# Two weight sums of a seven-product group made by accumulating transfers instead of a VectorE add, with four units loaded ahead and two more places for weights

## The chip, the cores and the metric

One core of one Trainium2 chip. The metric is the device time of one execution in microseconds (us); the kernel before was run three times for it. A profiled execution of the same program gives the trace that the views below are taken from.

## The reference, cut to what matters

A decoder layer on 256 tokens of width 2048, in float32:

```python
def swiglu(x, w_gu, w_down):
    g, u = jnp.split(x @ w_gu, 2, axis=-1)
    return (jax.nn.silu(g) * u) @ w_down

h = layer_norm(alpha * h + 0.5 * swiglu(h, w_ffn1_gu, w_ffn1_down), ...)
...   # token mixers: retention, windowed attention, their projections
h = layer_norm(alpha * h + mixed, ...)
h = layer_norm(alpha * h + 0.5 * swiglu(h, w_ffn2_gu, w_ffn2_down), ...)
ple = jax.nn.sigmoid(h @ w_ple_gate) * (p @ w_ple_proj)
h = layer_norm(alpha * h + ple, ...)
```

The change lies in the two products `x @ w_gu` (2048 by 11264 weights each), which the kernel calls `f1_gu` and `f2_gu`.

## The kernel before, in words

Every float32 operand is split in two parts, a high part rounded to the matmul's own type by a cast (`hi`) and the rest (`lo`); a product is then three matmuls, `al*bh + ah*bh + ah*bl` (`Sum.add`, lines 410 to 412). One matmul streams 512 columns.

**Blocks and units.** A gate and up product is cut into 11 blocks of output columns, each with 8 units of weights. A unit is 1 MB: four blocks of weights, 128 rows by 512, in one slot of 128 x 2048 float32. A plain unit (`Unit`, letter P) makes 8 products, 24 matmuls. A group of seven (`Seven`, letter S) makes the same result with 7 products, 21 matmuls, by a scheme of Strassen's kind: it needs sums of weight blocks and sums of activations. Block 0 has eight P; blocks 1 to 10 have four of each, in an order written out in `ORDERS`, mostly `PPSSPSSP`. The sevens of a block have `p` = 0 to 3 in that order, the plain ones 4 to 7.

**The work for one unit.** SyncE loads the unit with two transfers (`Unit.load`, line 200). For P, ScalarE casts it (`hf_gu`, line 204) and VectorE subtracts (`lf_gu`, line 208). For S, ScalarE casts three of the four weight blocks (`hbf_gu`, line 236). VectorE then makes four sums `u`: two with one add of 1024 elements (line 243), `u0 = b1 + b0` and `u1 = b2 + b0`, and one each at lines 247 and 248. ScalarE casts the sums in two halves (`huf_gu`, lines 244 and 249). VectorE makes the low parts `lb` (line 253, 1536 elements) and `lu` (line 257, 2048 elements). The add at 243 needs only the loaded blocks, and `lb` stands between the add at 248 and `lu`.

**What sets the order.** Each engine runs its instructions in the order in which the program emits them, and a planner in the kernel sets that order. It keeps two clocks, one for TensorE and one for VectorE (`spend` adds the time of an operation), and emits the steps of making a unit whenever the VectorE clock is behind. `load()` issues loads up to `room["far"]` units ahead, as far as `room["slots"]` places allow; `cast()` emits the next unit's first cast ahead of its turn where a place is free. `weights(n)` sets the number of places for each stage. All tiles of weights share a pool of 23 slots (`SLOTS`); in a gate and up block the planner is given `SLOTS - 5 - (j + 1) // 2` of them, 17 at block 1 and 13 at block 9, and two fewer in block 10. The rest hold the activation forms of the sevens (two slots), the block's output `eve` (one), the finished activations (`raws`, one for each two blocks).

**The end of a block.** At the last seven of a block the four auxiliary sums in PSUM are folded (`seven_common`): ScalarE copies one (line 496), VectorE does three operations (lines 499 to 501). Four pairs of PSUM banks are in rotation, and the next block's first matmuls write the pair that the fold reads last. Then VectorE adds the other two sums (line 831), ScalarE takes the silu (line 833), VectorE multiplies (line 836), and in the next block TensorE transposes the result (line 789) and ScalarE copies it out (line 790).

Of the kernel before, what the change touches and what calls it, by code (L numbers as in the profile page):

```python
# [8 lines left out]
F32 = mybir.dt.float32  # L9
F32R = mybir.dt.float32r  # L10
I32 = mybir.dt.int32
AF = mybir.ActivationFunctionType
ALU = mybir.AluOpType
PSUM = bass.MemoryType.PSUM

P = 128
S = 256
# [9 lines left out]
KF = FF // P  # L27
# [3 lines left out]
SLOTS = 23  # L31
# [65 lines left out]
    "b0, c0 b1, c1,, t0, t1,",  # L97
)

BIG = 3.0e38  # L100
MAGIC = 12582912.0
INV_2PI = 0.15915494309189535
# [20 lines left out]
def layer(ctx: ExitStack, tc: tile.TileContext, io):  # L123
    nc = tc.nc
    sync, act, dve, pe = nc.sync, nc.scalar, nc.vector, nc.tensor
# [3 lines left out]
    slots = ctx.enter_context(tc.tile_pool(name="slots", bufs=SLOTS))  # L129
# [7 lines left out]
    def slot(shape, dt, name):  # L137
        return slots.tile(shape, dt, tag="slot", name=name)
# [6 lines left out]
    plan = []  # L145
    GROUP_AT = {"rg": 8, "gr": 21, "ga": 29}

    class Place:


        def __init__(self, key):
            name, b, p = key
            self.grouped = True
            if name.endswith("_gu"):
                self.parts = [io[name][2 * b + c, :, p // 2, :, p % 2 * 2 : p % 2 * 2 + 2, :] for c in range(2)]
            elif name in GROUP_AT or name in ("w_ret", "w_att"):
                w, at = (io["w_in_f"], GROUP_AT[name]) if name in GROUP_AT else (io[name], 0)
                at += 4 * b
                self.parts = [w[at + c : at + 4 : 2, p // 2, :, p % 2 * 2 : p % 2 * 2 + 2, :] for c in range(2)]
            else:  # L160
                self.grouped = False
                self.parts = [io[name][2 * b + c, p] for c in range(2)]
# [9 lines left out]

        def piece(self, v, g, kk):
            return self.halves(v)[:, g, kk] if self.grouped else v[:, 2 * g + kk]

        def whole(self, raw):
            for c, src in enumerate(self.parts):
# [3 lines left out]
    def quarters(v):  # L181
        return v.rearrange("p j (c n) -> p j c n", c=2)

    class Unit:


        loads, makes, keeps, steps = 1, 2, 2, 1
# [9 lines left out]
        def load(self):  # L197
            self.tile()
            for dst, src in self.place.whole(self.raw):
                sync.dma_start(dst, src)  # L200
# [5 lines left out]
        def make(self):  # L206
            self.lo = slot([P, 4, 512], F32R, "l" + self.name)
            dve.tensor_tensor(self.lo, self.raw, self.hi, ALU.subtract)  # L208
            spend(2048)
            yield  # L210
# [18 lines left out]
    class Seven(Unit):  # L229


        loads, makes, keeps, steps = 1, 4, 4, 4
# [5 lines left out]
        def make(self):  # L238
            raw, hb, nm = self.place.blocks(self.raw), self.hb, self.name
            u = slot([P, 4, 512], F32, "u" + nm)  # L240
            hu = slot([P, 4, 512], F32R, "hu" + nm)
            at = quarters(u)
            dve.tensor_tensor(at[:, 0:2], raw[:, 1:3], raw[:, 0:1].broadcast_to([P, 2, 2, 256]), ALU.add)  # L243
            act.copy(hu[:, 0:2], u[:, 0:2])  # L244
            spend(1024)
            yield
            dve.tensor_tensor(at[:, 2], raw[:, 2], at[:, 0], ALU.add)
            dve.tensor_tensor(at[:, 3], at[:, 2], raw[:, 3], ALU.add)  # L248
            act.copy(hu[:, 2:], u[:, 2:])  # L249
            spend(512, 512)  # L250
            yield
            lb = slot([P, 3, 512], F32R, "lb" + nm)
            dve.tensor_tensor(quarters(lb), raw[:, 1:], quarters(hb), ALU.subtract)  # L253
            spend(1536)
            yield
            lu = slot([P, 4, 512], F32R, "lu" + nm)
            dve.tensor_tensor(lu, u, hu, ALU.subtract)  # L257
            spend(2048)
            self.b22, self.b11, self.b21 = ((hb[:, j], lb[:, j]) for j in range(3))
            self.t3, self.t1, self.t2, self.t4 = ((hu[:, j], lu[:, j]) for j in range(4))  # L260
            yield


# [1 line left out]
    clock = {"pe": 0.0, "dve": 0.0}  # L265
    loaded, making, ready = [], [], []
    beside = {}
    room = {"slots": 0, "used": 0, "far": 3}

    def spend(*sizes):  # L270
        for n in sizes:
            clock["dve"] += (n + 150) / 960
# [70 lines left out]
    def weights(n):  # L343
        room["slots"] = n
# [77 lines left out]
                    sums[t][c].add(half_of(lhs(2 * p + kk), t), u.piece(c, kk))  # L422

    def plan_block(name, b, units):
        plan.extend((Seven if kind == "S" else Unit)(name, b, p) for kind, p in units)

    def sums_of(ps, units):

# [7 lines left out]
    def block(name, b, units, lhs, forms, sums, fold, before=None, host=False):  # L436
        sevens = [p for kind, p in units if kind == "S"]
        aux = None
        for j, (kind, p) in enumerate(units):
            if before is not None:  # L440
                before(j)
            u = take(name, b, p)
            if kind == "P":
                for c in range(2):
                    for kk in range(2):
                        some_products(u, p, lhs, sums, (0, 1), (c,), (kk,))
                    if host and not c:
                        run_side()
                done(u)
                if (aux is None or not sevens) and j < len(units) - 1:  # L450
                    run_side()
                continue
            if aux is None:
                pair = [banks(f"{name}{b}s{j}") for j in range(2)]
                aux = p1, p6, p7, q5 = [Sum(pair[j // 2][:, j % 2], len(sevens)) for j in range(4)]
            a11, a12 = (half_of(lhs(2 * p + e), 0) for e in range(2))
            a22 = half_of(lhs(2 * p + 1), 1)
            f5, f6, f7, f3 = forms(p)
            q2, q3, q4 = sums[0][1], sums[0][0], sums[1][1]
            steps = [  # L460
                (p1, a11, u.b11), (q2, a12, u.b21), (q3, f3, u.b22), (q5, f5, u.t1),
                (p7, f7, u.t3), (p6, f6, u.t2), (q4, a22, u.t4),
            ]
            if p == sevens[-1]:
                steps = [steps[j] for j in (0, 3, 5, 4, 1, 2, 6)]
            for to, left, right in steps:
                to.add(left, right)
            done(u)
            if p == sevens[-1]:
                fold(*(x.ap for x in aux))  # L470
                sevens = []
# [301 lines left out]
    def ffn(name, i, ht, norm, keep, residual, keepers, away):  # L773
# [26 lines left out]
        for j in range(KF // 4):  # L800
            units = gu_units(name, j)
            if j:
                weights(SLOTS - 5 - (j + 1) // 2 - (2 if j == KF // 4 - 1 else 0))
            got = []
            offset = 0
            if norm is not None and j == 0:
                ps, sums = norm.front(name + "_gu", 0, rhs, units)
                offset, units = FRONT, units[FRONT:]
            else:
                ps = [banks(f"{name}g{j}{t}") for t in range(2)]  # L810
                sums = sums_of(by_half(ps), units)

            def before(u, j=j, offset=offset):
                u += offset
                if j == 3 and norm is None and u == 0:
                    load_constants()
                if j == 0 and norm is None and u == 6:
                    weights(12)
                if j == 0 and u == 7:
                    to = [slot([P, 16, P], F32R, f"{name}f{w}") for w in "hl"]  # L820
                    made["x"] = seven_forms(keep(), to)
                if j == KF // 4 - 1 and u in (4, 6):
                    convert(u // 2 - 2)

            block(name + "_gu", j, units, rhs, forms, sums, lambda *a: got.append(seven_common(*a)), before)
            if got:
                v = got[0]
                after()
                spend(1024, 1024)
                for t in range(2):  # L830
                    dve.tensor_tensor(v[:, 2 * t : 2 * t + 2], v[:, 2 * t : 2 * t + 2], ps[t], ALU.add)
                g, u = v[:, 0::2], v[:, 1::2]
                act.activation(g, g, AF.Silu)
                after(clock["dve"] + 1.3)
                spend(1024)
                dve.tensor_tensor(u, g, u, ALU.mult)
            else:
                v = slot([P, 4, 512], F32, f"{name}v{j}")
                u = v[:, 0::2]
                for t in range(2):  # L840
                    act.activation(v[:, 2 * t], ps[t][:, 0], AF.Silu)
                after(clock["pe"] + 1.2)
                spend(512, 512)
                for t in range(2):
                    dve.tensor_tensor(v[:, 2 * t], v[:, 2 * t], ps[t][:, 1], ALU.mult)
            later(1, lambda j=j, u=u: turned(j, u))
# [44 lines left out]
        units = second + [("P", p) for p in held]  # L891
# [779 lines left out]
```

## Time and profile before

| | |
|---|---|
| median of 3 runs | 2252.04 us (2251.95 to 2252.23) |
| the profiled execution's own time | 2252.07 us |
| its span, first to last instruction | 2250.2 us |
| TensorE busy | 2242.8 us |
| VectorE busy | 2025.6 us |
| ScalarE busy | 1221.1 us |
| GpSimd busy | 0.7 us |
| transfers | 465.31 MB, 207 GB/s over the span |

Busy time is a sum over instructions; TensorE's matmuls overlap one another in the pipeline, so that its busy time counts the time in which at least one is under way. Idle time of an engine that is not the bottleneck costs nothing. The DMA share is the mean busy share of the core's 16 DMA engines.

### The profile page before, as it was taken

The page shows a single profiled execution, that of the slowest core. Times are in us where ns is not written, and L with a number is a line of the kernel's source. Part 1 is how long each engine was busy: PE and PEld are TensorE (multiplying, and loading weights), DVE is VectorE, ACT ScalarE, POOL GpSimd, SP SyncE. Part 2 cuts the span into 40 slices and gives each one's busy share as a digit, 9 for nine tenths or more (in the row PEclk, how much of TensorE's full clock was granted, in tenths as well). Part 3 has the DMA queues.
Part 4 walks back from the last instruction along what each step waited for, and adds up shares of the span by engine and source line. Part 5 has one row for each costly group of instructions (what it writes and reads, how often), then busy time and mean ns, then how long its engine had stood idle before and what let it go on. Part 6 is the DMA issues. An engine that isn't in the chain of part 4 may idle for free.

```text
span 2250.2 us, 26572 instructions
## 1 busy us (share of the span) xinstructions
PE 2242.8 (100%) x10435; PEld 1870.6 (83%) x10435; DVE 2025.6 (90%) x1778; ACT 1221.1 (54%) x1030; POOL 0.7 (0%) x7
## 2 busy tenths in 40 slices
PE   9999999999999999999999999999999999999999
PEld 7888888888888888888888888888888888888887
DVE  7999999999997888899899878989999999989976
ACT  6655555555554455555555545455555566565542
POOL 0000000000000000000000000000000000000000
PEclk9999999999999999999999999999999999999999
DMA  8665665555577454355566665766566566555761
GB/s 318 206 214 179 214 206 186 190 204 206 210 271 264 166 221 150 137 197 193 168 210 220 195 215 195 271 230 216 174 206 213 185 201 207 187 213 214 281 268 70
DMA packets 189981, 465.31 MB, mean 207 GB/s; under 512 B 14368, under 2 KB 15904, under 8 KB 187296
## 3 DMA queue, kind: packets, MB, share of 16 engines
q1 hardware_dynamic: 188880, 462.43, 59.6%
q8 instruction: 82, 1.34, 0.2%
q10 hardware_dynamic: 976, 1.18, 0.2%
q14 instruction: 43, 0.35, 0.0%
HBM read 455.17 MB, written 8.39 MB: 206 GB/s over the span
## 4 chain that ended last, share of the span: by engine, by line
PE 99%; DMA 0%; DVE 0%; SPq 0%; ACT 0%; issue 0%; DVEq 0%; ACTq 0%
PE f1g L412 5%; PE f1g L410 5%; PE f1g L411 5%; PE f2g L411 4%; PE f2g L412 4%; PE f2g L410 4%; PE rqk L371 3%; PE aqk L371 2%; PE f2d L412 1%; PE f1d L411 1%; PE f2d L410 1%; PE f1d L410 1%; PE f1d L412 1%; PE f2d L411 1%; PE rqk L379 1%; PE f2e L412 1%
## 5 line engine op out<-in xcount | busy, mean ns | idle before, releaser
L208 DVE TENSOR_TENSOR lf_gu<-rf_gu,hf_gu 128x2048 fp32r<-128x2048 f32 x93 | 209.4, 2286 | 8.4 <-ACT hf_gu L204 8.4
L204 ACT CAST hf_gu<-rf_gu 128x2048 fp32r<-128x2048 f32 x93 | 175.9, 1909 | 34.4 <-DMA rf_gu<-in_f_gu 18.4
L257 DVE TENSOR_TENSOR luf_gu<-uf_gu,huf_gu 128x2048 fp32r<-128x2048 f32 x80 | 182.8, 2285 | 1.1 <-ACT huf_gu L249 1.1
L244 ACT CAST huf_gu<-uf_gu 128x1024 fp32r<-128x1024 f32 x80 | 84.2, 1053 | 141.8 <-DVE uf_gu L243 139.7
L412 PE MATMUL f1g<-lf_gu,xt 128*128 128x512 f32 x384 | 149.7, 390 | 0.5 <-DVE lf_gu L142 0.5
L410 PE MATMUL f1g<-hf_gu,xt 128*128 128x512 f32 x384 | 150.1, 391 | 0.1
L411 PE MATMUL f1g<-hf_gu,xt 128*128 128x512 f32 x384 | 149.7, 390 | 0.0
L208 DVE TENSOR_TENSOR lf_down<-rf_down,hf_down 128x2048 fp32r<-128x2048 f32 x60 | 136.2, 2287 | 13.5 <-ACT hf_down L204 5.5
L236 ACT CAST hbf_gu<-rf_gu 128x1536 fp32r<-128x1536 f32 x80 | 117.2, 1483 | 55.1 <-DMA rf_gu<-in_f_gu 40.2
L253 DVE TENSOR_TENSOR lbf_gu<-rf_gu,hbf_gu 128x1536 fp32r<-128x1536 f32 x80 | 140.1, 1751 | 0.0
L204 ACT CAST hf_down<-rf_down 128x2048 fp32r<-128x2048 f32 x60 | 114.3, 1913 | 47.5 <-DMA rf_down<-in_f_down 14.2
L410 PE MATMUL f2g<-hf_gu,ht 128*128 128x512 f32 x320 | 124.7, 390 | 0.0
L412 PE MATMUL f2g<-lf_gu,ht 128*128 128x512 f32 x320 | 124.7, 390 | 0.0
L411 PE MATMUL f2g<-hf_gu,ht 128*128 128x512 f32 x320 | 124.6, 390 | 0.0
L249 ACT CAST huf_gu<-uf_gu 128x1024 fp32r<-128x1024 f32 x80 | 84.2, 1052 | 34.2 <-DVE uf_gu L248 34.1
L243 DVE TENSOR_TENSOR uf_gu<-rf_gu 128x1024 f32<-128x1024 f32 x80 | 97.5, 1219 | 0.0
L412 PEld LDWEIGHTS f1g<-lf_gu,xt 128*128 128x128 f32 x384 | 72.1, 188 | 16.1 <-DVE lf_gu L142 1.2
L410 PEld LDWEIGHTS f1g<-hf_gu,xt 128*128 128x128 f32 x384 | 72.2, 188 | 15.3 <-ACT hf_gu L141 0.6
L411 PEld LDWEIGHTS f1g<-hf_gu,xt 128*128 128x128 f32 x384 | 72.3, 188 | 14.9
L257 DVE TENSOR_TENSOR luf_down<-uf_down,huf_down 128x2048 fp32r<-128x2048 f32 x28 | 64.0, 2287 | 7.8 <-ACT huf_down L249 5.9
L411 PEld LDWEIGHTS f2g<-hf_gu,ht 128*128 128x128 f32 x320 | 60.1, 188 | 12.4
L410 PEld LDWEIGHTS f2g<-hf_gu,ht 128*128 128x128 f32 x320 | 60.1, 188 | 12.4
(1331 smaller groups left out, 6418.6 us busy)
## 6 DMA issues: line engine op xcount, KB each, us to landing
rf_gu<-in_f_gu SPq DMA_DIRECT2D x350, 512.0 KB, 5.2
rf_down<-in_f_down SPq DMA_DIRECT2D x176, 512.0 KB, 4.5
rw_rv<-in_w_rv SPq DMA_DIRECT2D x32, 512.0 KB, 4.4
rrg<-in_w_in_f SPq DMA_DIRECT2D x32, 512.0 KB, 4.6
rgr<-in_w_in_f SPq DMA_DIRECT2D x32, 512.0 KB, 4.6
rw_ret<-in_w_ret SPq DMA_DIRECT2D x32, 512.0 KB, 5.0
rga<-in_w_in_f SPq DMA_DIRECT2D x32, 512.0 KB, 5.0
rw_mix<-in_w_mix SPq DMA_DIRECT2D x32, 512.0 KB, 4.5
```

Of the source, the lines that this page charges most:

```text
L204: act.copy(self.hi, self.raw)
L208: dve.tensor_tensor(self.lo, self.raw, self.hi, ALU.subtract)
L236: act.copy(quarters(self.hb), self.place.blocks(self.raw)[:, 1:])
L243: dve.tensor_tensor(at[:, 0:2], raw[:, 1:3], raw[:, 0:1].broadcast_to([P, 2, 2, 256]), ALU.add)
L244: act.copy(hu[:, 0:2], u[:, 0:2])
L249: act.copy(hu[:, 2:], u[:, 2:])
L253: dve.tensor_tensor(quarters(lb), raw[:, 1:], quarters(hb), ALU.subtract)
L257: dve.tensor_tensor(lu, u, hu, ALU.subtract)
L371: pe.matmul(ps[:, f], u.tile_of(kk)[0][:, f * P : (f + 1) * P], rhs(k), start=k == 0, stop=k == KD - 1,)
L410: pe.matmul(o, al, bh, start=first, stop=False)
L411: pe.matmul(o, ah, bh, start=False, stop=False)
L412: pe.matmul(o, ah, bl, start=False, stop=self.left == 0)
```

## The change

Sevens with `p` = 0 and `p` = 2 of `f1_gu` and `f2_gu` become `Summed`: two of the four in each of the ten blocks that have sevens, in both products, 40 units in all. Instead of the add at line 243, `u0` and `u1` are loaded as `b1` and `b2` by SyncE into a slot of their own, and two accumulating transfers issued by GpSimd add `b0` to each. `raw` then gets only `b1` to `b3`. In `make` the low part `lb` comes first and `lu` follows the second cast of the sums at once. `room["far"]` goes from 3 to 4 for the whole program, and each gate and up block after the first gets two more places; `SLOTS` stays at 23.

```diff
+SUMMED = [(name, p) for name in ("f1_gu", "f2_gu") for p in (0, 2)]
...
+        def block(self, g, kk):
+            name, b, p = self.key
+            if name.endswith("_gu"):
+                return io[name][2 * b : 2 * b + 2, g, p // 2, :, p % 2 * 2 + kk].rearrange("c p n -> p c n")
...
+        def half(self, g):
+            name, b, p = self.key
+            at = slice(p % 2 * 2, p % 2 * 2 + 2)
+            if name.endswith("_gu"):
+                return io[name][2 * b : 2 * b + 2, g, p // 2, :, at].rearrange("c p k n -> p c (k n)")
...
+    class Summed(Seven):
+        loads, makes, keeps, steps = 2, 3, 4, 3
+
+        def load(self):
+            self.tile()
+            self.u = slot([P, 4, 512], F32, "u" + self.name)
+            at, blocks = quarters(self.u), self.place.blocks(self.raw)
+            for j, place in enumerate(((0, 1), (1, 0))):
+                sync.dma_start(at[:, j], self.place.block(*place))
+            for j in range(2):
+                nc.gpsimd.dma_start(at[:, j], self.place.block(0, 0), accum_op=ALU.add)
+            sync.dma_start(blocks[:, 1], self.place.block(0, 1))
+            if self.place.grouped:
+                sync.dma_start(self.raw[:, 1::2], self.place.half(1))
+            else:
+                sync.dma_start(self.raw[:, 2:], self.place.parts[1])
+
+        def make(self):
+            raw, hb, nm, u = self.place.blocks(self.raw), self.hb, self.name, self.u
+            at = quarters(u)
+            lb = slot([P, 3, 512], F32R, "lb" + nm)
+            dve.tensor_tensor(quarters(lb), raw[:, 1:], quarters(hb), ALU.subtract)
+            spend(1536)
+            yield
+            hu = slot([P, 4, 512], F32R, "hu" + nm)
+            act.copy(hu[:, 0:2], u[:, 0:2])
+            dve.tensor_tensor(at[:, 2], raw[:, 2], at[:, 0], ALU.add)
+            dve.tensor_tensor(at[:, 3], at[:, 2], raw[:, 3], ALU.add)
+            act.copy(hu[:, 2:], u[:, 2:])
+            spend(512, 512)
+            yield
+            lu = slot([P, 4, 512], F32R, "lu" + nm)
+            dve.tensor_tensor(lu, u, hu, ALU.subtract)
+            spend(2048)
+            self.parts(hb, lb, hu, lu)
             yield
...
-    room = {"slots": 0, "used": 0, "far": 3}
+    room = {"slots": 0, "used": 0, "far": 4}
...
-        plan.extend((Seven if kind == "S" else Unit)(name, b, p) for kind, p in units)
+        for kind, p in units:
+            plan.append((Unit if kind == "P" else Summed if (name, p) in SUMMED else Seven)(name, b, p))
...
-                weights(SLOTS - 5 - (j + 1) // 2 - (2 if j == KF // 4 - 1 else 0))
+                weights(SLOTS - 3 - (j + 1) // 2 - (2 if j == KF // 4 - 1 else 0))
```

`parts` only names the finished tiles, as the end of `Seven.make` did.

More of the change, by code (lines that the diff above doesn't have):

```diff
@@ L151, in __init__ @@
         def __init__(self, key):
+            self.key = key
             name, b, p = key
@@ L174, in piece @@
             return self.halves(v)[:, g, kk] if self.grouped else v[:, 2 * g + kk]
+        def block(self, g, kk):
+            name, b, p = self.key
+            if name.endswith("_gu"):
+                return io[name][2 * b : 2 * b + 2, g, p // 2, :, p % 2 * 2 + kk].rearrange("c p n -> p c n")
+            if not self.grouped:
+                return self.parts[g][:, kk].rearrange("p (c n) -> p c n", c=2)
+            w, at = (io["w_in_f"], GROUP_AT[name]) if name in GROUP_AT else (io[name], 0)
+            at += 4 * b + 2 * g
+            return w[at : at + 2, p // 2, :, p % 2 * 2 + kk].rearrange("c p n -> p c n")
+        def half(self, g):
[3 more added lines that the diff above has]
+                return io[name][2 * b : 2 * b + 2, g, p // 2, :, at].rearrange("c p k n -> p c (k n)")
+            w, n = (io["w_in_f"], GROUP_AT[name]) if name in GROUP_AT else (io[name], 0)
+            n += 4 * b + 2 * g
+            return w[n : n + 2, p // 2, :, at].rearrange("c p k n -> p c (k n)")
         def whole(self, raw):
@@ L258, in make, with parts @@
             spend(2048)
+            self.parts(hb, lb, hu, lu)
+            yield
+        def parts(self, hb, lb, hu, lu):
             self.b22, self.b11, self.b21 = ((hb[:, j], lb[:, j]) for j in range(3))
             self.t3, self.t1, self.t2, self.t4 = ((hu[:, j], lu[:, j]) for j in range(4))
+    class Summed(Seven):
[26 more added lines that the diff above has]
+            spend(512, 512)
+            yield
+            lu = slot([P, 4, 512], F32R, "lu" + nm)
+            dve.tensor_tensor(lu, u, hu, ALU.subtract)
+            spend(2048)
+            self.parts(hb, lb, hu, lu)
             yield
```

## The prediction

> **What bounds the kernel now.** I read the page first, then the table of windows over the blocks of both gate and up products, then the waits of TensorE and of SyncE's queue, and last the timeline of VectorE and ScalarE through one change of blocks.
>
> ```profile
> span 2250.2 us, 26572 instructions
> PE 2242.8 (100%) x10435; PEld 1870.6 (83%) x10435; DVE 2025.6 (90%) x1778; ACT 1221.1 (54%) x1030; POOL 0.7 (0%) x7
> ...
> PE 99%; DMA 0%; DVE 0%; SPq 0%; ACT 0%; issue 0%; DVEq 0%; ACTq 0%
> ```
>
> ```profile
> PE idle L1551 <- POOL ident masks.py:199: 1.4, 1, 1.4
> PE pls L1484 <- DVE ends L1481: 1.2, 1, 1.2
> PE f1g L412 <- DVE lf_gu L142: 0.5, 1, 0.5
> ```
>
> The chain that ends last is 99% TensorE. TensorE is idle for 2250.2 - 2242.8 = 7.4 us in all, and the second fence, all its named waits, adds up to 3.1 us: at the start (L1551, L142) and in the last norm (L1484). The change touches none of them. The windows say the same of the place of the change (columns: stretch, length, then busy time and count of each engine, clock, DMA share, GB/s):
>
> ```profile
> 61.40:103.10 41.70, 41.70 (x192) 34.65 (x189) 41.29 (x31) 23.86 (x20) 0.00 (x0) 1.00 0.61 202
> ...
> sum 418.60, PE 418.60 PEld 347.81 DVE 402.40 ACT 239.75 POOL 0.00; mean PE 41.86 PEld 34.78 DVE 40.24 ACT 23.98 POOL 0.00
> ```
>
> ```profile
> sum 418.10, PE 418.10 PEld 347.41 DVE 398.82 ACT 238.88 POOL 0.00; mean PE 41.81 PEld 34.74 DVE 39.88 ACT 23.89 POOL 0.00
> ```
>
> The first row is one block, the sums are ten stretches in `f1_gu` and ten in `f2_gu`. TensorE is busy in all of each, at clock 1.00. VectorE is the second engine: 402.40 of 418.60 and 398.82 of 418.10, so 1.6 to 1.9 us free in each block. It keeps pace, but only just. The change alters no matmul. What it can do is keep TensorE fed or starve it; it cannot shorten it.
>
> **The add that goes, and the wait that comes.**
>
> ```profile
> L257 DVE TENSOR_TENSOR luf_gu<-uf_gu,huf_gu 128x2048 fp32r<-128x2048 f32 x80 | 182.8, 2285 | 1.1 <-ACT huf_gu L249 1.1
> L244 ACT CAST huf_gu<-uf_gu 128x1024 fp32r<-128x1024 f32 x80 | 84.2, 1053 | 141.8 <-DVE uf_gu L243 139.7
> ...
> L243 DVE TENSOR_TENSOR uf_gu<-rf_gu 128x1024 f32<-128x1024 f32 x80 | 97.5, 1219 | 0.0
> ```
>
> Forty of the eighty adds at 243 go: 40 x 1.219 = 48.8 us of VectorE, two in a block, 2.44 us. The order of the rest matters more than it looks. Timeline of VectorE, then of ScalarE, around the change from block 9 to 10 (start, length):
>
> ```profile
> 419.77 0.69 DVE L499 TENSOR_TENSOR eve<-eve,f_gu9s 128x512 f32<-128x512 f32 x1
> ...
> 421.28 1.22 DVE L501 TENSOR_TENSOR eve<-f_gu9s,eve 128x1024 f32<-128x1024 f32 x1
> 422.42 1.22 DVE L243 TENSOR_TENSOR uf_gu<-rf_gu 128x1024 f32<-128x1024 f32 x1
> 424.47 2.35 DVE L831 TENSOR_TENSOR eve<-eve,f1g 128x1024 f32<-128x1024 f32 x2 [0.83 <-PE f1g L412]
> ...
> 433.08 1.22 DVE L243 TENSOR_TENSOR uf_gu<-rf_gu 128x1024 f32<-128x1024 f32 x1
> 434.33 0.69 DVE L247 TENSOR_TENSOR uf_gu<-rf_gu,uf_gu 128x512 f32<-128x512 f32 x1
> 435.05 0.69 DVE L248 TENSOR_TENSOR uf_gu<-uf_gu,rf_gu 128x512 f32<-128x512 f32 x1
> 435.66 1.75 DVE L253 TENSOR_TENSOR lbf_gu<-rf_gu,hbf_gu 128x1536 fp32r<-128x1536 f32 x1
> 437.33 2.29 DVE L257 TENSOR_TENSOR luf_gu<-uf_gu,huf_gu 128x2048 fp32r<-128x2048 f32 x1
> 439.53 1.22 DVE L243 TENSOR_TENSOR uf_gu<-rf_gu 128x1024 f32<-128x1024 f32 x1
> ```
>
> ```profile
> 417.77 1.49 ACT L236 CAST hbf_gu<-rf_gu 128x1536 fp32r<-128x1536 f32 x1 [3.89 <-DMA rf_gu<-in_f_gu]
> 419.16 0.58 ACT L496 COPY eve<-f_gu9s 128x512 f32<-128x512 f32 x1
> ...
> 435.78 1.05 ACT L249 CAST huf_gu<-uf_gu 128x1024 fp32r<-128x1024 f32 x1 [0.34 <-DVE uf_gu L248]
> ```
>
> Now a seven takes VectorE from 433.08 to 439.53, 6.45 us. The second cast of the sums (L249) starts when the add at 248 is done and ends at 435.78 + 1.05 = 436.83; it is hidden under `lb` (L253), which is why `lu` has waited for it 1.1 us in total over 80. In `Summed`, `lb` comes first, so nothing lies between the add at 248 and `lu`: VectorE, free at 435.66, would wait until 436.83, 1.17 us. By these rows 40 x 1.17 = 46.8 us come back, and the net is 48.8 - 46.8 = 2 us of VectorE over twenty blocks: nothing. VectorE stays as loaded as before. The low bound of that wait is 0 (another step emitted there fills it), giving the full 2.44 us a block; the high bound adds a cast of the next unit that stands ahead on ScalarE, 1.49 us by L236. I take 1.17. The planner's own clock does not count the wait.
>
> The casts of ScalarE are the same in number; the first now waits for a transfer instead of L243.
>
> **Bytes.** A seven loads 4 blocks of 0.262 MB. A `Summed` loads two of them again and one twice by accumulation: 5 plain and 2 accumulating, +0.262 MB plain and +0.524 MB accumulating. In a block of two that is +0.52 and +1.05 MB; over 40 units HBM reads rise by 31.5 MB.
>
> ```profile
> 21.00:52.00 31.00, 31.00 (x139) 25.68 (x138) 25.81 (x18) 16.91 (x11) 0.00 (x0) 1.00 0.90 323
> ```
>
> A block now uses 0.61 of 41.7 us, 25.4 us, for 202 GB/s, so full use is 202 / 0.61 = 331 GB/s; this stretch near the start ran at 0.90 and 323 GB/s with TensorE busy throughout. At 331 GB/s the extra takes 1.58 us plain and 3.17 us if accumulating bytes cost as plain ones: share 0.72. No row shows an accumulating transfer, so the other end is where it saturates: 41.7 - 25.4 - 1.6 = 14.7 us for 1.05 MB, 71 GB/s, 4.6 times dearer than plain. I take a share between 0.72 and 0.80, the second if each such byte costs twice. The Trainium skill, "Collectives: The Full Stack", section "The bandwidth ceiling: the fold count and why AG ≠ RS ≠ AR", says that an adding transfer is slower not for the sum but for its two source reads, half the rate; by it the share is 0.80, and no run here shows it yet.
>
> **When the data is there.** Transfers and waits of SyncE:
>
> ```profile
> rf_gu<-in_f_gu ACTq DMA_DIRECT2D x2, 256.0 KB, 3.7
> rf_gu<-in_f_gu SPq DMA_DIRECT2D x2, 256.0 KB, 5.2
> ...
> L200 SPq DMA_DIRECT2D rf_gu<-in_f_gu x4: 368/418/470, 412.0 to 413.5; - x4
> ...
>   ACT hbf_gu L236: 5.0, 2
> ...
> DMA to landing us min/median/max: 3.8/5.6/7.3
> ```
>
> The last three rows are two units loaded from 412.0 on, the first of them a seven with `p` = 0, which will be `Summed`. Its add started at 422.42. `Summed` needs the sums one `lb` later, at about 424.1, 12.1 us after the load is issued. The chain: one issue of 0.42, a landing of 3.7 to 5.2, two issues on GpSimd (0.42 each as on SyncE, the nearest row), again 3.7 to 5.2: 8.7 to 11.7 us, in time. With 7.3 for each landing it is 15.9, 3.8 us late. Issue on GpSimd has no row; its low end is 0.42, and the chain bears 2.2 us for each with landings of 3.7. So no wait in my sum, 3.8 us at the far end.
>
> On SyncE four issues stand where two stood: 2 x 0.42 = 0.84 us more, and 0.262 MB more at 331 GB/s, 0.79 us; `raw` is complete 1.6 us later. Behind it in ScalarE's order wait the cast at 417.77 and the copy at 419.16 (L496), and behind that the fold, which ended at 421.28 + 1.22 = 422.50. The block's own first sum was complete only at 424.47, where L831 had waited 0.83 us for TensorE, and the next block writes the fold's banks after that. So the fold has 2.0 us to spare, and 1.6 leaves 0.4. Price on the path: 0, but this is the thinnest cover.
>
> **Places.** The pool keeps 23 slots, so "two more places" is room that lay unused in the planner's count, and a `Summed` in flight holds a slot more from load to `make`. With at most two in flight that is even: 0. `far` = 4 acts in every stage; a fourth load can take the place of a cast ahead, and VectorE then waits for that cast, as it already does now and then (idle before, last column):
>
> ```profile
> L208 DVE TENSOR_TENSOR lf_gu<-rf_gu,hf_gu 128x2048 fp32r<-128x2048 f32 x93 | 209.4, 2286 | 8.4 <-ACT hf_gu L204 8.4
> ```
>
> 8.4 us for 93 units, and even twice that is spread over two products and lies in VectorE's free time. 0, at most some 5 us.
>
> **Sum.** TensorE's path 2250.2 + 0 = 2250.2 us of span. The profiled execution took 2252.07, 1.9 more, and stands 0.03 above the median. Forecast 2252 us, no change; for this likeliest case 2249 to 2256.5. A measurement here can tell 0.2%, 4.5 us, from no change.
>
> **The rivals.**
> 1. Late sums or late folds: the wait moves to TensorE. Place: the first `Summed` of a block, its landing against ScalarE's copy L496 or the first cast of sums. It decides from the point where the fold is over 2.0 us later or VectorE loses over 1.6 to 1.9 us a block. With landings of 7.3 us, 3.8 - 1.7 = 2.1 us a block, 42 us, 2294; with half a microsecond a block, 10 us, 2262. For it: ScalarE already waits for the landing of such units (3.89 us), and VectorE gains nothing. Against: the second `Summed` of a block has more time, and loading further ahead may bring the first forward. Typical 2265.
> 2. The DMA engines saturate. Under 71 GB/s for accumulating bytes a block needs more than 41.7 us; at 50 GB/s 25.4 + 1.6 + 21.0 = 48.0, +6.3 us, 126 us over twenty blocks, 2378. Against: the engines have 39% free and two reads would leave 20%.
> 3. Writing descriptors on GpSimd holds VectorE. GpSimd is idle now (0.7 us). If each of four transfers a block stopped VectorE for its issue, 0.42 us by SyncE's row, the 1.7 us that are free would just cover it; at 1.25 us each it is 5.0 - 1.7 = 3.3 us a block, 66 us, 2318. Nearly all VectorE work here is two-input TENSOR_TENSOR. The Trainium skill, "SBUF — State Buffer", section "Who interferes with whom", has such an operation contend with GpSimd instructions that read SBUF, and infers that writing descriptors is not one; no run here shows it.
> 4. The change does less than it says, `far` = 4 alone acting: a few us of TensorE waits in the mixers, 2258.
> 5. Faster: TensorE's idle time is 7.4 us, so 2252.07 - 7.4 = 2244.7 is the floor, and none of it lies in the blocks; a gain of 4.6 us, 2247.5, would need most of it.
>
> **How the numbers follow.** No change 0.54. Rival 1 0.27, rival 2 0.07, rival 3 0.05, rival 4 0.05, rival 5 0.02. So faster 0.02, same 0.54, slower 0.44. The range goes from 2249 to 2282: it takes in the forecast, rival 4 and most of rival 1, and leaves out the far end of 1, and 2 and 3, under 0.2.
>
> **What the profile after would show.** Right: TensorE busy again for all of each block window; 40 instead of 80 adds at 1024 elements; `lu` of `Summed` waiting about 1.2 us for ScalarE's second cast, some 40 to 47 us in total, and VectorE's busy time down by 48.8; DMA share 0.72 to 0.80 in the blocks; GpSimd with 80 transfers. Wrong: TensorE waits on `luf_gu`, `huf_gu` or on the fold at the first matmuls of a block (rival 1), a DMA share near 1 (rival 2), longer VectorE operations beside GpSimd's work (rival 3). What would overturn the forecast is an accumulating transfer dearer or later than the plain rows say.

## The result, and the profile after

| | before | after |
|---|---|---|
| median of 4 runs | 2251.99 us (2251.80 to 2252.23) | 2389.15 us (2386.64 to 2394.14) |
| ratio | 1 | 1.0612, 95% interval 1.0592 to 1.0632 |
| the profiled execution's own time, span | 2252.07, 2250.2 us | 2394.14, 2392.4 us |

The change costs 137 us. The time after is outside the range of the prediction.

The functions moved down in the file: `Sum.add` is now at lines 478 to 480, a plain unit's cast and `lo` at 228 and 232, the old seven's operations at 260 to 281, `Summed`'s at 302 (SyncE), 304 (GpSimd), 315 (`lb`), 319 (first cast), 320 and 321 (sums), 322 (second cast) and 326 (`lu`), the fold at 565 to 570. The first lines of the page of the changed kernel, its two DMA queues (packets, MB, share) and its memory traffic:

```profile
span 2392.4 us, 26998 instructions
PE 2296.6 (96%) x10435; PEld 1890.4 (79%) x10435; DVE 1988.1 (83%) x1738; ACT 1220.0 (51%) x1030; POOL 98.9 (4%) x87
...
q1 hardware_dynamic: 210640, 472.92, 57.6%
q0 software_dynamic: 21760, 20.98, 5.8%
HBM read 486.62 MB, written 8.39 MB: 207 GB/s over the span
```

VectorE does less (2025.6 to 1988.1 us), the DMA engines are far from full, and TensorE executes the same 10435 matmuls. It is no longer busy all the time: idle 2392.4 - 2296.6 = 95.8 us where 7.4 were. That is 88.4 of the 142.2 us by which the span grew. The other 53.8 are busy time, the same matmuls taking longer. Windows over blocks 0 to 9 of the first product, from the transposes of block 0 to those of block 10, before and then after (columns: length, busy of TensorE, weight loads, VectorE, ScalarE, GpSimd, granted clock, DMA share, GB/s):

```profile
60.60:477.50 416.90, 416.90 (x1881) 346.41 (x1880) 402.30 (x300) 239.16 (x190) 0.00 (x0) 1.00 0.61 201
```

```profile
60.60:535.80 475.20, 438.32 (x1881) 354.25 (x1880) 385.89 (x280) 242.63 (x192) 44.15 (x36) 0.96 0.71 211
```

The same stretch of work takes 58.3 us longer. Of these 36.9 are idle and 21.4 busy, at a granted clock of 0.96. The same stretch of the second product grew by 60.6 us; the remaining 23 us lie mostly in the mixers between the two. What TensorE waited for, after (us in total, times, longest):

```profile
PE f1g L478 <- DVE eve L568: 19.5, 8, 5.0
PE f2g L478 <- DVE eve L568: 19.1, 6, 5.7
PE f1g L478 <- DVE eve L570: 8.7, 9, 1.1
PE f2g L478 <- DVE eve L570: 6.2, 8, 1.1
PE w_rv1s L480 <- DVE luw_rv L281: 3.5, 1, 3.5
PE w_mix1s L480 <- DVE lbw_mix L277: 2.9, 1, 2.9
```

The four largest, 53.5 us together, are one place: the first matmuls of a block, waiting for the fold of the block before. None of the larger waits is for weights of a `Summed`. Two more kinds, 15.9 us in seven waits, belong to the end of a block too: once the transposes wait for the other two sums (line 900), and six times matmuls of a seven in blocks 3, 4 and 6 wait for ScalarE's copy of the transposed result (line 859), as in

```profile
PE f2t L858 <- DVE eve L900: 2.9, 1, 2.9
PE f_gu3s L478 <- ACT f1a L859: 2.3, 1, 2.3
```

So the question is why the fold is late. VectorE's timeline around the fold of block 5, before and then after (start, length, engine, line, operation, in brackets the idle time before it and what ended it):

```profile
243.62 2.29 DVE L257 TENSOR_TENSOR luf_gu<-uf_gu,huf_gu 128x2048 fp32r<-128x2048 f32 x1
245.82 6.69 DVE L208 TENSOR_TENSOR lf_gu<-rf_gu,hf_gu 128x2048 fp32r<-128x2048 f32 x3
252.42 0.68 DVE L499 TENSOR_TENSOR eve<-eve,f_gu5s 128x512 f32<-128x512 f32 x1
```

```profile
262.79 2.29 DVE L232 TENSOR_TENSOR lf_gu<-rf_gu,hf_gu 128x2048 fp32r<-128x2048 f32 x1 [1.64 <-ACT hf_gu L228]
265.00 1.75 DVE L315 TENSOR_TENSOR lbf_gu<-rf_gu,hbf_gu 128x1536 fp32r<-128x1536 f32 x1
...
269.52 2.29 DVE L326 TENSOR_TENSOR luf_gu<-uf_gu,huf_gu 128x2048 fp32r<-128x2048 f32 x1 [1.45 <-ACT huf_gu L322]
271.73 1.22 DVE L267 TENSOR_TENSOR uf_gu<-rf_gu 128x1024 f32<-128x1024 f32 x1
...
275.99 2.28 DVE L281 TENSOR_TENSOR luf_gu<-uf_gu,huf_gu 128x2048 fp32r<-128x2048 f32 x1
278.19 0.68 DVE L568 TENSOR_TENSOR eve<-eve,f_gu5s 128x512 f32<-128x512 f32 x1
...
293.65 1.76 DVE L315 TENSOR_TENSOR lbf_gu<-rf_gu,hbf_gu 128x1536 fp32r<-128x1536 f32 x1 [5.99 <-PE f1g L479]
```

Before, three plain units stand ahead of the fold and the sevens of the next group come behind it. After, a whole `Summed` and a whole old seven stand ahead of it as well, with a wait for a cast in them. ScalarE's copy that the fold needs was made earlier, by 275.97 (275.39 + 0.58, ScalarE's timeline after); the fold started at 278.19, when VectorE came to it.

```profile
275.39 0.58 ACT L565 COPY eve<-f_gu5s 128x512 f32<-128x512 f32 x1
```

VectorE's row at 293.65 shows the other side of it: VectorE had run so far ahead that it then stood idle for 5.99 us until TensorE freed a slot. TensorE's timeline at the same moment:

```profile
273.57 0.39 PE L480 MATMUL f1g<-lf_gu,xt 128*128 128x512 f32 x1
278.93 0.69 PE L478 MATMUL f1g<-hf_gu,xt 128*128 128x512 f32 x1 [4.97 <-DVE eve L568]
...
281.56 0.63 PE L479 MATMUL f1g<-hf_gu,xt 128*128 128x512 f32 x1
281.99 0.63 PE L480 MATMUL f1g<-lf_gu,xt 128*128 128x512 f32 x1
...
286.33 0.40 PE L479 MATMUL f1g<-hf_gu,xt 128*128 128x512 f32 x1
286.56 0.40 PE L480 MATMUL f1g<-lf_gu,xt 128*128 128x512 f32 x1
```

It waits for 4.97 us, and the matmuls behind the wait start 0.43 us apart, until 285.8, where they start 0.23 us apart: half speed for about 7 us. Most of the 53.8 us of extra busy time is this: the granted clock of the profiled run is 0.981, and 0.019 of 2392.4 us are about 45 us.

How many units VectorE has finished when it comes to the fold can be counted in its timeline (`lf` and `lu` rows, first product). Every kernel below that loses over 15 us in the blocks has a later row than the kernel before, and every one that loses less has the same row; how much is lost, the row alone does not tell:

| kernel | units finished ahead of the fold of blocks 1 to 10 |
|---|---|
| before | 23, 31, 39, 47, 55, 63, 71, 79, 87, 93 |
| after | 24, 32, 40, 48, 57, 65, 72, 80, 88, 93 |

### The profile page after: what moved, and what is told of

Same layout as the page of the kernel before. It is cut to its first block, busy times and chain, and to the rows that moved or that the text cites. A ratio compares the mean times of both kernels' runs of the same rounds, so it can differ in the third digit from the quotient of the medians.

```text
span 2392.4 us, 26998 instructions
## 1 busy us (share of the span) xinstructions
PE 2296.6 (96%) x10435; PEld 1890.4 (79%) x10435; DVE 1988.1 (83%) x1738; ACT 1220.0 (51%) x1030; POOL 98.9 (4%) x87
## 3 DMA queue, kind: packets, MB, share of 16 engines
q1 hardware_dynamic: 210640, 472.92, 57.6%
q0 software_dynamic: 21760, 20.98, 5.8%
HBM read 486.62 MB, written 8.39 MB: 207 GB/s over the span
## 5 line engine op out<-in xcount | busy, mean ns | idle before, releaser
L478 PE MATMUL f1g<-hf_gu,xt 128*128 128x512 f32 x384 | 156.1, 407 | 28.2 <-DVE eve L568 19.5
L304 POOL DMA_DIRECT2D uf_gu<-in_f_gu x80 | 98.2, 1428 | 1908.3 <-DMA rf_gu<-in_f_gu 1181.2
L478 PE MATMUL f2g<-hf_gu,ht 128*128 128x512 f32 x320 | 131.2, 410 | 25.3 <-DVE eve L568 19.1
L479 PE MATMUL f1g<-hf_gu,xt 128*128 128x512 f32 x384 | 154.4, 402 | 0.0
L326 DVE TENSOR_TENSOR luf_gu<-uf_gu,huf_gu 128x2048 fp32r<-128x2048 f32 x40 | 91.7, 2293 | 60.4 <-ACT huf_gu L322 54.7
L479 PE MATMUL f2g<-hf_gu,ht 128*128 128x512 f32 x320 | 129.4, 404 | 0.0
L478 PEld LDWEIGHTS f1g<-hf_gu,xt 128*128 128x128 f32 x384 | 74.9, 195 | 52.0 <-DVE eve L568 23.3
L478 PEld LDWEIGHTS f2g<-hf_gu,ht 128*128 128x128 f32 x320 | 62.9, 197 | 45.6 <-DVE eve L568 22.1
L268 ACT CAST huf_gu<-uf_gu 128x1024 fp32r<-128x1024 f32 x40 | 42.0, 1051 | 92.3 <-DVE uf_gu L267 86.6
L479 PEld LDWEIGHTS f1g<-hf_gu,xt 128*128 128x128 f32 x384 | 74.8, 195 | 15.1
L277 DVE TENSOR_TENSOR lbf_gu<-rf_gu,hbf_gu 128x1536 fp32r<-128x1536 f32 x40 | 70.1, 1752 | 15.9 <-PE f2g L480 5.8
L902 ACT ACTIVATE eve<-eve 128x1024 f32<-128x1024 f32 x20 | 21.2, 1062 | 116.2 <-DVE eve L900 116.2
```

What stands on the lines that cost most here:

```text
L304: nc.gpsimd.dma_start(at[:, j], self.place.block(0, 0), accum_op=ALU.add)
L478: pe.matmul(o, al, bh, start=first, stop=False)
L479: pe.matmul(o, ah, bh, start=False, stop=False)
```

## The experiments

Two theories were tested first. A: the two settings, with their two more places, let the planner emit one or two more units ahead of each fold. B: the transfers are late, or the uncovered second cast (`lb` first) is in the way. The first four kernels below refuted both as the main cause. Theory C came after them: `Summed` no longer calls `spend(1024)` for the add, 2 x 1.22 = 2.44 us a block, so the planner's VectorE clock falls behind sooner and one or two more units are emitted ahead of the folds. Its rival D was the load path of `Summed`: a second slot from the load on, more bytes, a later `raw`. Every ratio is to the kernel before on the same chip.

**The settings alone**, on the kernel before:

```diff
-    room = {"slots": 0, "used": 0, "far": 3}
+    room = {"slots": 0, "used": 0, "far": 4}
...
-                weights(SLOTS - 5 - (j + 1) // 2 - (2 if j == KF // 4 - 1 else 0))
+                weights(SLOTS - 3 - (j + 1) // 2 - (2 if j == KF // 4 - 1 else 0))
```

> The kernel before with far = 4 and two more places (SLOTS - 3), all sevens as they were, no accumulating transfer. Theory A (places): the planner puts one or two more units ahead of each fold, VectorE then waits in its order for slots that TensorE frees later, and the fold is late; most of the 137 us come back here, 2330 to 2390, with TensorE waits on the fold at block starts. Theory B (accumulating transfers late, or the cast of the sums in the way of lu): no Summed, so 2250 to 2258.

Measured: 2273.74 us, 1.0096 (1.0081 to 1.0111), 21.7 us, in neither range. The blocks take 41.7 us each and the folds stand as before. The loss is in the mixers (the stages between the two products); windows of this kernel and of the kernel before, and its two longest waits of TensorE:

```profile
720.00:1450.00 730.00, 716.22 (x3512) 599.22 (x3511) 628.99 (x662) 383.40 (x375) 0.00 (x0) 0.99 0.56 191
```

```profile
720.00:1450.00 730.00, 730.00 (x3609) 615.16 (x3608) 642.18 (x680) 392.54 (x380) 0.00 (x0) 1.00 0.58 197
```

```profile
PE w_rv1s L412 <- DVE luw_rv L257: 3.5, 1, 3.5
PE w_mix1s L412 <- DVE lbw_mix L253: 2.9, 1, 2.9
```

In the same 730 us 97 fewer matmuls are done. These are the two waits that the changed kernel has too. So the settings are worth about 22 of the 137 us, in stages where only `far` = 4 differs.

**`Summed` without the settings** (the changed kernel with `far` = 3 and `SLOTS - 5`):

> The 40 Summed with their accumulating transfers, but far = 3 and SLOTS - 5 as before. Theory A: at most a few us, 2250 to 2270, since the places are as before. Theory B: most of the loss, 2330 to 2390, since the late sums and the uncovered second cast are all there; places fewer by two could make it worse still, over 2390.

Measured: 2407.78 us, 1.0691 (1.0673 to 1.0709), slower still, far from the 2250 to 2270 of theory A. The folds stand one and two units later as in the changed kernel, and with fewer places the loads are late too. The settings help `Summed` in the blocks by more than they cost in the mixers.

**The accumulating transfers left out**, with all else as after, so that `b0` is missing from two sums:

```diff
-            for j in range(2):
-                nc.gpsimd.dma_start(at[:, j], self.place.block(0, 0), accum_op=ALU.add)
```

> The changed kernel without the 80 accumulating transfers: u0 and u1 keep b1 and b2 alone, so the sums lack b0 and that part of the computation is left out. Everything else, order, places and the other loads, is the same. Theory A (places, order): within 20 us of the changed kernel, 2370 to 2390. Theory B in the form of late transfers: 2255 to 2290. DMA share in the blocks falls from about 0.73 to about 0.65 in either.

Measured: 2368.37 us, 1.0516, 20.8 us less than after. 116 us are lost without one accumulating transfer, so late transfers are not the main cause.

**`lb` between the sums and `lu`**, which covers the second cast again:

```diff
-            lb = slot([P, 3, 512], F32R, "lb" + nm)
-            dve.tensor_tensor(quarters(lb), raw[:, 1:], quarters(hb), ALU.subtract)
-            spend(1536)
-            yield
             hu = slot([P, 4, 512], F32R, "hu" + nm)
...
             spend(512, 512)
             yield
+            lb = slot([P, 3, 512], F32R, "lb" + nm)
+            dve.tensor_tensor(quarters(lb), raw[:, 1:], quarters(hb), ALU.subtract)
+            spend(1536)
```

> The changed kernel with lb again between the sums and lu in Summed, so that the second cast of the sums is covered. The waits of lu on ScalarE, 54.7 us, should fall under 15. Theory A: VectorE gains up to 40 us over twenty blocks but the fold still stands behind too many units, 2350 to 2385. Theory B in the form of the uncovered cast: 2255 to 2300. The sums are now needed one lb earlier, which could cost up to 1.7 us for each late landing.

Measured: 2349.59 us, 1.0433 (1.0412 to 1.0454), 39.6 us less than after. The wait that was to fall under 15 us fell from 54.7 to 21.6; VectorE's waits of the changed kernel and of this one:

```profile
DVE luf_gu L326 <- ACT huf_gu L322: 54.7, 38, 3.2
```

```profile
DVE luf_gu L326 <- ACT huf_gu L318: 21.6, 17, 2.9
```

Still 97 us are lost, though VectorE here is nearly as quick as the planner counts. The folds stand as in the changed kernel.

**The count alone, on the kernel before**: all operations as before, but the add not counted for the 40 units.

```diff
-            spend(1024)
+            if self.key[0] not in ("f1_gu", "f2_gu") or self.key[2] not in (0, 2):
+                spend(1024)
```

> The kernel before, far = 3 and SLOTS - 5, all sevens as they were, with one edit: for the 40 sevens with p = 0 and 2 of the gate and up products the planner no longer counts the add of 1024 (no spend(1024)). VectorE's work and all transfers are unchanged. Theory C (the planner's clock): the planner takes VectorE for 2.4 us a block faster than it is, puts one or two more units ahead of the fold, as in the changed kernel (24, 32, 40, 48, 57, 65 units made before the folds, against 23, 31, 39, 47, 55, 63), and the fold is late: 2290 to 2370. Rival D (the load path of Summed: a second slot from load on, more bytes, later raw): nothing of that is here, 2250 to 2258.

Measured: 2274.95 us, 1.0095 (1.0079 to 1.0112). Nothing but the order changed, with folds at 24, 32, 40, 48, 56, 64, 72, and 22.9 us are lost. This is less than the 2290 at which theory C's range began: in the kernel before, the count alone is not worth the whole loss.

**The count put back, in the changed kernel**:

```diff
-            spend(512, 512)
+            spend(1024, 512, 512)
```

> The changed kernel with spend(1024) added in Summed.make, so that the planner counts as much VectorE time for a Summed as for a Seven, which is what it really takes with the uncovered cast. Theory C: the folds stand behind 23, 31, 39 ... units again and the blocks return to 41.7 to 44 us; 2275 to 2310, of which 20 are far = 4 in the mixers. Rival D: no gain, 2370 to 2400.

Measured: 2274.55 us, 1.0097 (1.0077 to 1.0117): 114.6 of the 137 us are back by one number, and the rest, 22.5, is what the settings alone cost. The folds stand at 23, 31, 39, 47, 55, 63, the blocks take 41.7 us, and the accumulating transfers, the extra slot and the uncovered cast are all still there. **With `lb` between as well:**

> As e6, with lb between the sums and lu again, so that VectorE really is 2.4 us a block faster than the planner thinks. Theory C: 2272 to 2285, which leaves the 20 us of far = 4. Rival D: 2330 to 2390.

Measured: 2273.52 us, 1.0093 (1.0072 to 1.0113), the same. The uncovered cast costs 39.6 us where the fold is late and nothing where it is in place. **And with `far` = 3 everywhere:**

> As e7 with far = 3. If the 21.7 us of the settings alone are far = 4 in the mixers, this is 20 us under e7: 2252 to 2265 by theory C, and the accumulating transfers by themselves cost nothing. Rival D: 2310 to 2390, since loading less far ahead makes the sums later.

Measured: 2264.47 us, 1.0051 (1.0036 to 1.0066). The mixers are as before, but block 0 to block 1 takes 47.06 us, and a few others 43: `Summed` needs the fourth unit ahead in its blocks.

**The fold ahead of the planner's pump**: to move the fold forward without the count, the `pump` at its head was taken out.

```diff
-        pump(clock["pe"] - 15 * MATMUL)
...
-        after()
+        clock["dve"] = max(clock["dve"], clock["pe"])
```

> The changed kernel with one edit in seven_common: the fold is emitted at once, without first emitting further making steps (no pump before it; the planner's VectorE clock is only set to TensorE's). The planner's clock stays as in the changed kernel, which counts no add for a Summed. Theory C, sharpened (it is the units put ahead of the fold that make it late): the fold stands behind fewer units again and most of the 115 us that paying the clock recovered come back, 2275 to 2310. If the loss is rather in the units themselves (their slots, their late sums), 2350 to 2390.

Measured: 2391.79 us, 1.0619. A miss that says nothing on the theory: the folds stand where they stood, at 24, 32, 40, 48, 57, 65, because the units ahead of them are emitted earlier than that call.

**The early slot**: settings and folds of the changed kernel, but the 40 units load with plain transfers and do the add (uncounted) in the old order; only the slot for `u` is still taken at the load.

```diff
-            for j, place in enumerate(((0, 1), (1, 0))):
-                sync.dma_start(at[:, j], self.place.block(*place))
...
+            for dst, src in self.place.whole(self.raw):
+                sync.dma_start(dst, src)
...
+            dve.tensor_tensor(at[:, 0:2], raw[:, 1:3], raw[:, 0:1].broadcast_to([P, 2, 2, 256]), ALU.add)
             dve.tensor_tensor(at[:, 2], raw[:, 2], at[:, 0], ALU.add)
```

> The changed kernel with no extra transfer: the 40 units load as plain sevens and VectorE makes their two sums with the add of 1024 as before, in the old order, but the slot for the sums is taken from the load on (loads 2, makes 3), and the planner still does not count that add. So it is e5 with the settings and the places of the changed kernel. If the early slot costs nothing: settings 21.7 and clock 22.7 add up, 2296. If it is the early slot that turns the 23 us of e5 into 115: 2330 to 2390.

Measured: 2334.55 us, 1.0365 (1.0346 to 1.0384). No accumulating transfer and no saved add, and 82.6 us are lost, with the folds at the row of the changed kernel (24, 32, 40, 48, 57, 65, ...). The settings (21.7) and the count (22.9) apart make 44.6. The other 38.0 come when the early slot stands beside these two; which of the three it takes is not shown.

**The repaired version**: count put back, `lb` between, `far` = 4 only in gate and up blocks after block 0.

```diff
+            room["far"] = 4 if 0 < j else 3
...
+        room["far"] = 3
```

> As e7 (clock paid, lb between the sums and lu) with far = 4 only in the gate and up blocks with sevens and far = 3 elsewhere. By theory C and the place of e1's loss (the mixers) this is the kernel before again: 2251 to 2256, with the accumulating transfers and 31 MB more of traffic hidden. It cannot be faster by over 3 us, since TensorE was never idle there.

Measured: 2258.68 us, 1.0029 (1.0018 to 1.0039). This is 2.7 us above the expected range: block 0 to block 1 of the first product takes 47.0 us, the rest is level.

**One unit more ahead of the fold, nothing else changed**, on the kernel before, the test of the theory by itself:

```diff
+            def fold_later(*a):
+                n = len(ready)
+                while len(ready) == n and step():
+                    pass
+                got.append(seven_common(*a))
+
-            block(name + "_gu", j, units, rhs, forms, sums, lambda *a: got.append(seven_common(*a)), before)
+            block(name + "_gu", j, units, rhs, forms, sums, fold_later, before)
```

> The kernel before with one edit: in the gate and up blocks one more unit is made ahead of each fold (the planner steps until another unit is ready, then folds). Clock, places, loads and all work as before. Theory C (the fold behind one more unit in VectorE's order is what delays it): the units made before the folds are 24, 32, 40 ... as in e5 and the time is 2265 to 2340. If the place of the fold does not matter and the loss needs the planner's clock in another way: 2250 to 2258.

Measured: 2299.64 us, 1.0211 (1.0193 to 1.0230), 47.6 us. VectorE's timeline at the fold of block 5 in this kernel (L249 is the second cast of the sums):

```profile
244.83 6.69 DVE L208 TENSOR_TENSOR lf_gu<-rf_gu,hf_gu 128x2048 fp32r<-128x2048 f32 x3
251.44 1.22 DVE L243 TENSOR_TENSOR uf_gu<-rf_gu 128x1024 f32<-128x1024 f32 x1
...
257.69 2.29 DVE L257 TENSOR_TENSOR luf_gu<-uf_gu,huf_gu 128x2048 fp32r<-128x2048 f32 x1 [1.86 <-ACT huf_gu L249]
259.90 0.68 DVE L499 TENSOR_TENSOR eve<-eve,f_gu5s 128x512 f32<-128x512 f32 x1
```

One seven has slipped in between the three plain units and the fold, which starts at 259.90 instead of 252.42. About 2.0 of these 7.48 us were there before: the transposes at the start of the block come at 229.34 instead of 227.37. The block takes 43.7 us instead of 41.7. **The same edit on the changed kernel with the count put back:**

> e6 (the changed kernel with the clock paid, 2274.5) with one more unit made ahead of each gate and up fold. Theory C: most of the 115 us that paying the clock won are lost again, 2330 to 2400, and more than e12 loses, since here no slot lies idle and the units ahead wait for slots that TensorE has still to free. If the place of the fold does not matter: 2270 to 2285.

Measured: 2332.89 us, 1.0359 (1.0340 to 1.0378), 58.3 us above the kernel that it was made from. The folds stand at 24, 32, 40, 48, 56, 64, and TensorE waits at the same place as in the changed kernel:

```profile
PE f1g L478 <- DVE eve L568: 11.1, 6, 3.3
PE f2g L478 <- DVE eve L568: 8.9, 4, 3.3
```

**The repaired version from block 0 on** (`far` = 4 in every gate and up block, 3 elsewhere):

```diff
+            room["far"] = 4
...
+        room["far"] = 3
```

> e11 with far = 4 from block 0 of each gate and up product on. In e11 only the stretch from block 0 to 1 of the first product was longer (47.0 us against 41.7 before and 42.0 in e6, which has far = 4 there). So 2251 to 2255: level with the kernel before, with the 80 accumulating transfers in it. Not faster: TensorE has nothing to gain.

Measured: 2252.51 us (11 runs, 2252.07 to 2252.68), 1.0002 (0.9993 to 1.0011): level with before, with all 80 accumulating transfers in it. The kernel with `far` = 4 everywhere and otherwise the same took 2273.52, so `far` = 4 outside the gate and up blocks costs 21.0 us. Lines of its page, two blocks' windows, and rows of the tile `u` (nanoseconds min/median/max, first and last start):

```profile
PE 2243.4 (100%) x10435; PEld 1870.0 (83%) x10435; DVE 1980.6 (88%) x1738; ACT 1219.3 (54%) x1030; POOL 99.0 (4%) x87
q1 hardware_dynamic: 210640, 472.92, 61.0%
q0 software_dynamic: 21760, 20.98, 6.2%
```

```profile
61.40:103.10 41.70, 41.70 (x191) 34.62 (x190) 40.43 (x30) 23.63 (x19) 4.91 (x4) 1.00 0.81 240
395.00:436.60 41.60, 41.60 (x189) 34.52 (x188) 37.99 (x29) 22.20 (x18) 4.91 (x4) 1.00 0.88 259
```

```profile
L304 POOL DMA_DIRECT2D uf_gu<-in_f_gu x80: 1203/1280/1746, 39.1 to 1872.4; - x80
L317 DVE TENSOR_TENSOR uf_gu<-uf_gu,rf_gu x40: 691/692/694, 49.5 to 1891.3; 128x512 f32<-128x512 f32 x40
L326 DVE TENSOR_TENSOR luf_gu<-uf_gu,huf_gu x40: 2281/2284/2293, 51.8 to 1893.7; 128x2048 fp32r<-128x2048 f32 x40
```

No version beat the kernel before: TensorE was never idle in the blocks, so the 45.0 us taken off VectorE (2025.6 to 1980.6) shorten nothing.

**The sum of it.** Five kernels form a chain, the time of each beside the step to it:

| kernel | us | step |
|---|---|---|
| before | 2252.0 | |
| + the two settings | 2273.7 | +21.7 |
| + add not counted, slot taken at the load | 2334.6 | +60.8 |
| + transfers in place of the add | 2349.6 | +15.0 |
| + `lb` first: after | 2389.2 | +39.6 |

The same steps with the count put back come to +21.7 and then +0.8 for all the rest together. It is shown that the later steps cost only while the fold is late, and that one unit more ahead of each fold, with no other change, costs 47.6 us in one kernel and 58.3 in another. What sets the size of the loss is not shown. The kernel with the count alone has the same row of folds as these two and loses 22.9, and the other half of the 114.6 us was not made by itself. The changed kernel has the fold two units late at blocks 5 and 6 and also emits the joins (the sums at line 900) up to three units later, 58 instead of 55 at block 5. The 15.9 us of waits behind the joins and their transposes stand in neither kernel with one unit more ahead of the fold. Neither the second unit nor the joins were tried alone.

## Why the prediction was wrong, step by step

- **TensorE bounds the blocks and VectorE's saved time buys nothing**: right. The last kernel has VectorE down by 45.0 us and is level.
- **The uncovered second cast** (46.8 us over 40): right in kind, 54.7 us over 38 waits in the changed kernel, 29.0 over 29 with the count put back. That it leaves the time alone holds only with the fold in place; with the fold late it was worth 39.6.
- **"The planner's own clock does not count the wait"**: the step that failed. The clock was looked at, but only for the wait, and given no price. I took the order of the instructions as unchanged, and never followed the missing `spend(1024)` through it. With it gone, one or two more units stand ahead of nine of the ten folds of the first product; with the count put back, 114.6 of the 137 us are back.
- **The fold**, "2.0 us to spare", the "thinnest cover", price 0: the right place and the wrong cause. The lateness came from VectorE's own order, not from a load 1.6 us late. A unit placed ahead of it made the fold of block 5 7.48 us later in the kernel with that edit alone (252.42 to 259.90), some 5.5 of them in that block, over the 2.0.
- **Rival 1** (late folds) had the place right. I sized it at 10 to 42 us; the two products lost 58.3 + 60.6 = 118.9. The half speed behind many of these waits was in no term.
- **Places**, price 0: right with the count put back, where the slot taken at the load costs nothing that shows; wrong with the fold late, where slot, settings and uncounted add together cost 38.0 us more than settings and count apart.
- **Bytes**: HBM reads rose from 455.17 to 486.62 MB, the 31.5 forecast. Share of the engines 0.72 to 0.80 forecast; in the last kernel 0.79 and 0.78 over ten blocks of each product, 0.81 and 0.88 in the two blocks shown. An accumulating byte was taken at one to two times a plain one, with a bound of 4.6. By the queues' rows of the last kernel (20.98 MB at 6.2%, 472.92 at 61.0%) it is (6.2 / 20.98) / (61.0 / 472.92) = 2.3 times. Most plain packets are larger, though: among packets of 1 KB an accumulating one takes 107 ns in that trace and a plain one 50, 2.1 times. The Trainium skill, "Collectives: The Full Stack", section "The bandwidth ceiling: the fold count and why AG ≠ RS ≠ AR", has half the rate for the adding step of a collective, so twice the price; the measured 2.1 for packets of one size is near it.
- **Issue on GpSimd**: 1.28 us (median) where 0.42 was taken. It lies within the bound of 2.2 us that the chain was to bear, and cost nothing that shows with the count put back.
- **Rival 2** (saturation): false, with a share of 0.71 in the slow product and full speed at 0.81 and 0.88; that its 2378 is near the measured time is chance. **Rival 3** (descriptor writing holds VectorE): false. The adds of 512 take 691 to 694 ns with the transfers (line 317) and without (line 248 before). Of the 40 subtractions `lu` of the old sevens in the last kernel, 12 run while such an issue is under way and take 2280 to 2292 ns, the other 28 2281 to 2296. The rule of "SBUF — State Buffer", section "Who interferes with whom", in the Trainium skill agrees.
- **Rival 4** (`far` = 4 in the mixers): right in place, and 21.7 us where I gave 6.

## What to carry to other kernels

A planner's table of costs is part of the kernel: taking work off an engine that is not the bound can reorder that engine, so count, before and after, what stands ahead of each instruction that the bounding engine waits for. When a change moves the time, put the planner's count back first and judge the change with the old order. A depth of loading ahead is set for each stage, since here the same value was needed in one and cost 21 us in the others.

## What the runs showed of the hardware

Waits of TensorE can cost more than their length. Behind the 4.97 us wait shown above, the matmuls ran 0.43 us apart for about 7 us, then 0.23; over the changed kernel 88.4 us of added idle time went with 53.8 us of added busy time. The Trainium skill, "TensorE: Matmul & The Clock Gate", section "Part 1: The HAM clock gate (the "warmup" mystery)", has the rate halved after an idle window of about 3.4 us and given back after as much of busy time; that the rate halves agrees, and here the half rate lasted about twice that. The length of the wait does not agree: in the kernel before with one unit more ahead of the fold no wait of TensorE was over 1.9 us, and behind one of 1.88 us (before the matmul at 305.87) the granted clock, third number from the end in the window's row, was 0.50 all the same:

```profile
305.87 0.50 PE L410 MATMUL f1g<-hf_gu,xt 128*128 128x512 f32 x1 [1.88 <-DVE eve L499]
```

```profile
306.40:313.00 6.60, 5.86 (x14) 4.11 (x14) 6.39 (x8) 2.25 (x3) 0.00 (x0) 0.50 0.33 116
```

An accumulating transfer of 256 KB from GpSimd's queue landed a median of 6.8 us after its issue in the last kernel, a plain one into the same tile 5.3 (page, transfers by queue):

```profile
uf_gu<-in_f_gu SPq DMA_DIRECT2D x80, 256.0 KB, 5.3
uf_gu<-in_f_gu POOLq DMA_DIRECT2D x80, 256.0 KB, 6.8
```
